# Sums of weight quarters in a Strassen-like MLP product: accumulating DMAs in place of VectorE, with the seven products in another order

## The chip, the cores and the metric

The kernel runs on one core of one Trainium2 chip. The metric is device time in microseconds of one execution. Besides the time there is a trace of one profiled execution, with every instruction of the engines: TensorE (PE; its weight loads are counted apart as PEld), VectorE (DVE), ScalarE (ACT), GpSimd (POOL), and SyncE (SP), which here only issues DMAs. POOL and ACT can issue DMAs as well.

## What is computed

One layer of a hybrid decoder: 16 meta tokens and 512 sequence positions of width 1024 pass through pooling and a state-space branch, gates and an output product; then comes a squared-ReLU MLP, and a final normalisation. The change lies in the MLP:

```python
v = rmsnorm(h, mlp_norm_w[i])
hid = jax.nn.relu(v @ w_ff1[i])          # 512 x 4096 for the positions that are kept
h = h + (hid * hid) @ w_ff2[i]           # 4096 -> 1024
```

All of it is float32. The kernel takes each float32 matrix apart into a high part that PE multiplies fast (type fp32r) and a low remainder (`hi` and `lo`), and forms a product from three matmuls: high by high, high by low, low by high.

## The kernel before

All weights come as one DRAM tensor `w` of blocks of 128 x 1024 float32 (512 KB), laid out in the order in which the kernel takes them; `nblk[0]` counts the blocks taken. SP loads a block into one of three `raw` tiles (line 68); ACT casts it to `whi` (line 69) and DVE subtracts to `wlo` (line 70); there are four `whi` and four `wlo` tiles.

The MLP stage has two kinds of work, woven into each other.

- The first product: 32 tiles `ff1_tile(c, f)`, 24 matmuls of 128 x 512 each (lines 86 to 88) into a bank `pf`, then relu and square on ACT (lines 708, 709). After the fourth tile of a group `c`, sums and differences of its quarters are formed on DVE (lines 724 to 727), and everything is taken apart into `hh` and `hl`. Six tiles run ahead; the others serve as fillers (`filler()`) between the products below.
- The second product: the depth of 4096 is taken in eight slices `c`. For the first seven, the product of the two-by-two quarters of activations and weights is formed from seven products instead of eight (Winograd's form of Strassen's method). Each product is `prod(...)`, 12 matmuls of 128 x 512 (lines 742 to 744). Four quarters of weights are loaded per slice, by `quarter` (SP, line 685), into tiles of a pool of six: `b11`, `b12`, `b22`, `b21`. The trace calls them all `b`, and the third sum tile `t`. The seven right-hand sides are b11, b22 and b21 on their own and four sums: t1 = b11 + b12, t2 = t1 + b22, b12 + b22, and t2 + b21. The four sums are formed by DVE in `sum_of` (line 764). Each right-hand side goes through `split` (ACT line 692 into `shi`, DVE line 693 into `slo`, in the same four-deep pool as `whi` and `wlo`).

The products are named after the activations' side: A11, S2, S3, A22, S4, A12 and S1. A11, S2, S3 and A22 accumulate one onto another in the PSUM tile `alpha` (two banks); S4 starts `alpha` anew. After each of these five, DVE adds or subtracts `alpha` onto the result `ht` (`onto`, line 754). The next product in `alpha` can begin only after that. A12 accumulates over all slices in `p2` (shown as `p`), S1 in two banks `q5` (shown as `q`), which in the last of the seven slices is added onto `ht` by four operations of 512 columns. The eighth slice is an ordinary product (line 849), followed by the final normalisation and the store.

The order of each engine's instructions isn't the code's order. The framework plans it once, at build time: from its own costs it follows what each engine would be doing and gives it the earliest instruction in the code whose inputs and buffers it expects to be ready. On the chip each engine then keeps to that order and waits on semaphores; it cannot pass over an instruction that waits. A tile's buffer comes free when its last reader has finished. The text speaks of a block: one of the seven slices with its seven products and the fillers among them, four in blocks 1 to 5 and three in the sixth and the seventh.

Of the kernel before, what the change touches and what calls it, by code (L numbers as in the profile page):

```python
# [9 lines left out]
F32 = mybir.dt.float32  # L10
# [4 lines left out]
P = 128  # L15
# [30 lines left out]
def kernel(ctx: ExitStack, tc, xT, x, w, vec, fnw, out):  # L46
    nc = tc.nc
    act, dve, pe, pool = nc.scalar, nc.vector, nc.tensor, nc.gpsimd
# [8 lines left out]
    nblk = [0]  # L57
# [70 lines left out]
    def psum2(name):  # L128
        return psa.tile([P, 1024], F32, tag="mm", name=name)

    def psum1(name):
        return psb.tile([P, 512], F32, tag="s", name=name)
# [71 lines left out]
    for i in range(2):  # L204
        c = slice(i * HALF, (i + 1) * HALF)
# [11 lines left out]
    def dtile(name):  # L217
        return dp.tile([P, W], F32, name=name)

    v, e, s, s2, pl, dt, acs = (dtile(n) for n in ("dv", "de", "ds", "ds2", "dpl", "ddt", "dacs"))  # L220
# [22 lines left out]
    for c in (slice(0, P), slice(P, W)):  # L243
        n = c.stop - c.start
# [342 lines left out]
    for d in range(NK):  # L587
        ps = psum2(f"pup{d}")[:, :SEQ]
        wh, wl = block()
        for n, k in enumerate(ks):  # L590
            c = slice(k * P, (k + 1) * P)
# [35 lines left out]
    for half in range(2):  # L627
# [5 lines left out]
        for kk in range(4):  # L633
            wh, wl = block()
            for k2 in range(2):
                k = 2 * kk + k2
                c = slice(k2 * 512, (k2 + 1) * 512)
# [4 lines left out]
        c = slice(half * 512, (half + 1) * 512)  # L642
# [19 lines left out]
    qp = ctx.enter_context(tc.tile_pool(name="qp", bufs=6, side="left", reuse_waits="tile"))  # L662
# [14 lines left out]
    A12, A22, A11, S1, S2, S4, S3 = range(7)  # L677
    NC = 8
    rel = {}

    def quarter(tag):
        b = nblk[0]
        nblk[0] += 1
        t = qp.tile([P, 1024], F32, tag="quarter", name=f"{tag}{b}")
        nc.sync.dma_start(t, w[b])
        return t

    def split(src):
        hi = wp.tile([P, 1024], F32R, tag="whi", name=f"shi{nsplit[0]}")
        lo = wp.tile([P, 1024], F32R, tag="wlo", name=f"slo{nsplit[0]}")  # L690
        nsplit[0] += 1
        act.copy(hi, src)  # L692
        dve.tensor_tensor(lo, src, hi.bitcast(F32), op=ALU.subtract)  # L693
        return hi, lo
# [3 lines left out]
    def ff1_tile(c, f):  # L698
        ps = psum1(f"pf{c}_{f}")
        wh, wl = block()  # L700
        for k in range(NK):
            ks = slice(k * P, (k + 1) * P)
            mm3(ps, (wh[:, ks], wl[:, ks]), (vh[k], vl[k]), k == 0, k == NK - 1)
        if f == 0:
            rel[c] = tmp.tile([P, 2, 4, 256], F32, tag="relu", name=f"r{c}")
        p, i = f // 2, f % 2
        r = rel[c][:, p, 2 * i : 2 * i + 2, :].rearrange("p s t -> p (s t)")
        act.activation(r, ps, AF.Relu)
        act.activation(r, r, AF.Square)
        if f < 3:  # L710
            return
        r = rel[c]
        hh = hid.tile([P, 2, 7, 256], F32R, tag="hh", name=f"hh{c}")
        hl = hid.tile([P, 2, 7, 256], F32R, tag="hl", name=f"hl{c}")
        if c == NC - 1:
            act.copy(hh[:, :, :4, :], r)
            dve.tensor_tensor(hl[:, :, :4, :], r, hh[:, :, :4, :].bitcast(F32), op=ALU.subtract)
            rel[c] = (hh, hl)
            return

        act.copy(hh[:, :, :3, :], r[:, :, :3, :])
        dve.tensor_tensor(hl[:, :, :3, :], r[:, :, :3, :], hh[:, :, :3, :].bitcast(F32), op=ALU.subtract)
        s = tmp.tile([P, 2, 4, 256], F32, tag="sums", name=f"s{c}")
        dve.tensor_tensor(s[:, :, 0, :], r[:, :, 3, :], r[:, :, 1, :], op=ALU.subtract)
        dve.tensor_tensor(s[:, :, 1, :], s[:, :, 0, :], r[:, :, 2, :], op=ALU.subtract)
        dve.tensor_tensor(s[:, :, 2, :], r[:, :, 0, :], s[:, :, 1, :], op=ALU.add)
        dve.tensor_tensor(s[:, :, 3, :], r[:, :, 2, :], r[:, :, 3, :], op=ALU.subtract)
        act.copy(hh[:, :, 3:, :], s)
        dve.tensor_tensor(hl[:, :, 3:, :], s, hh[:, :, 3:, :].bitcast(F32), op=ALU.subtract)
        rel[c] = (hh, hl)  # L730

    def prod(ps, c, seg, wt, first, last, ts=(0, 1)):

        hh, hl = rel[c]
        wh, wl = wt
        for t in ts:
            for p in range(2):
                st = slice(t * P, (t + 1) * P)
                a = (hh[:, p, seg, st], hl[:, p, seg, st])
                cs = slice(p * 512, (p + 1) * 512)  # L740
                f, l = first and p == 0, last and p == 1
                pe.matmul(ps[t], a[0], wh[:, cs], start=f, stop=False, skip_group_check=True)  # L742
                pe.matmul(ps[t], a[0], wl[:, cs], start=False, stop=False, skip_group_check=True)  # L743
                pe.matmul(ps[t], a[1], wh[:, cs], start=False, stop=l, skip_group_check=True)  # L744

    def onto(T, half, pst, op, t=None):

        cs = slice(half * 512, (half + 1) * 512)
        if t is None:
            o = ht[:, 2 * T : 2 * T + 2, cs]  # L750
            src = pst.rearrange("p (t d) -> p t d", t=2)
        else:
            o, src = ht[:, 2 * T + t, cs], pst
        dve.tensor_tensor(o, o, src, op=op)  # L754

    ADD, SUB = ALU.add, ALU.subtract
    alpha, p2 = psum2("alpha"), psum2("p2")
    av = [alpha[:, :512], alpha[:, 512:]]
    p2v = [p2[:, :512], p2[:, 512:]]
    q5v = [psum1(f"q5_{t}") for t in range(2)]  # L760

    def sum_of(a, b, name, out=None):
        t = out if out is not None else qp.tile([P, 1024], F32, tag="quarter", name=name)
        dve.tensor_tensor(t, a, b, op=ADD)
        return t

    def squares(t, c, n):
# [23 lines left out]
    def filler():  # L791
        if order:
            ff1_tile(*order.pop(0))

    for c in range(NC - 1):
        b11, b12, b22, b21 = (quarter(n) for n in ("b11_", "b12_", "b22_", "b21_"))
        z, e = c == 0, c == NC - 2
        prod(av, c, A11, split(b11), True, False)
        onto(0, 0, alpha, ADD)
        t1 = sum_of(b11, b12, "", b11)  # L800
        t2 = sum_of(t1, b22, f"t2_{c}")
        filler()
        prod(av, c, S2, split(t2), False, False)
        onto(0, 1, alpha, SUB)
        filler()
        prod(av, c, S3, split(sum_of(b12, b22, "", b12)), False, False)
        onto(1, 1, alpha, SUB)
        filler()
        prod(av, c, A22, split(sum_of(t2, b21, "", t2)), False, True)
        onto(1, 0, alpha, ADD)  # L810
        if e:
            prod(q5v, c, S1, split(t1), z, True)
            for t in range(2):
                onto(0, 1, q5v[t], ADD, t)
                onto(1, 1, q5v[t], ADD, t)
        elif c < NC - 3:
            filler()
        prod(av, c, S4, split(b22), True, True)
        onto(0, 1, alpha, ADD)
        prod(p2v, c, A12, split(b21), z, False)  # L820
        if not e:
            prod(q5v, c, S1, split(t1), z, False)
    assert not order


    c = NC - 1
# [5 lines left out]
    for t in range(4):  # L832
        T, st = t // 2, slice((t % 2) * P, (t % 2 + 1) * P)
        n = 0
        for half in range(2):
            parts = [(0, 512)] if half == 0 or t < 3 else [(0, 256), (256, 256)]
            for a, m in parts:
# [4 lines left out]
                for k, seg in ((1, (A11, 3)[T]), (0, (A12, A22)[T])):  # L842
                    wh, wl = wq[k, half]
                    for p in range(2):
                        x0 = p * 512 + a
                        f = i == 0 and not (T == 0 and half == 0)
# [151 lines left out]
```

## Time and profile before

| | |
|---|---|
| median of 3 runs | 1034.95 us (1034.86 to 1035.31) |
| profiled execution | 1035.26 us |
| its span, first to last instruction | 1033.5 us |
| mean granted PE clock | 0.998 |
| busy: PE, PEld | 1019.6 us, 880.2 us |
| busy: DVE, ACT, POOL | 714.2 us, 542.3 us, 9.9 us |
| read from HBM | 102.95 MB |
| MLP stage, first filler to last matmul | 697.8 to 1028 us |

A line of the timeline gives an instruction's start and duration, the engine, the line of the code, the operation, the tiles written and read, and in brackets the idle time of the engine before it and what released it. Matmuls overlap in the pipeline: each shows 0.39 us but the next one starts 0.23 us later. A line of groups gives the same for all instructions of one kind, with their count and duration (least, median, most). A DMA's landing time counts from its issue to the moment that its data is there.

### The profile page before, as it was taken

The page shows a single profiled execution, that of the slowest core. Times are in us where ns is not written, and L with a number is a line of the kernel's source. Part 1 is how long each engine was busy: PE and PEld are TensorE (multiplying, and loading weights), DVE is VectorE, ACT ScalarE, POOL GpSimd, SP SyncE. Part 2 cuts the span into 40 slices and gives each one's busy share as a digit, 9 for nine tenths or more (in the row PEclk, how much of TensorE's full clock was granted, in tenths as well). Part 3 has the DMA queues.
Part 4 walks back from the last instruction along what each step waited for, and adds up shares of the span by engine and source line. Part 5 has one row for each costly group of instructions (what it writes and reads, how often), then busy time and mean ns, then how long its engine had stood idle before and what let it go on. Part 6 is the DMA issues. An engine that isn't in the chain of part 4 may idle for free.

```text
span 1033.5 us, 13995 instructions
## 1 busy us (share of the span) xinstructions
PE 1019.6 (99%) x5700; PEld 880.2 (85%) x5700; DVE 714.2 (69%) x932; ACT 542.3 (52%) x706; POOL 9.9 (1%) x24
## 2 busy tenths in 40 slices
PE   7999999999999999999999999999999999999997
PEld 7889988898879898988998888878888888888886
DVE  7978787687636586878664345645686676776866
ACT  7675968586627349573443123344555354454444
POOL 0100000000000000000000000000000000000000
PEclk9999999999999999999999999999999999999999
DMA  6343041414332321413232323533324323334112
GB/s 229 110 140 103 21 164 37 148 47 137 102 112 73 103 101 41 146 59 111 77 107 95 102 81 102 204 126 122 99 82 123 103 81 122 102 102 123 42 41 82
DMA packets 29424, 106.01 MB, mean 103 GB/s; under 512 B 3312, under 2 KB 4272, under 8 KB 28336
## 3 DMA queue, kind: packets, MB, share of 16 engines
q1 hardware_dynamic: 26640, 93.14, 28.8%
q0 software_dynamic: 2000, 11.08, 2.9%
q8 instruction: 45, 0.74, 0.3%
q10 hardware_dynamic: 720, 0.91, 0.3%
q14 instruction: 19, 0.16, 0.0%
HBM read 102.95 MB, written 2.16 MB: 102 GB/s over the span
## 4 chain that ended last, share of the span: by engine, by line
PE 97%; DVE 1%; DMA 1%; ACT 0%; issue 0%; SPq 0%; ACTq 0%
PE px L138 6%; PE px L141 6%; PE px L139 6%; PE pf L86 6%; PE pf L87 6%; PE pf L88 6%; PE alpha L742 3%; PE alpha L743 3%; PE alpha L744 3%; PE pz L139 3%; PE pz L141 3%; PE pz L138 3%; PE py L416 2%; PE pso L86 2%; PE pp L141 2%; PE pp L139 2%
## 5 line engine op out<-in xcount | busy, mean ns | idle before, releaser
L69 ACT CAST whi<-raw 128x1024 fp32r<-128x1024 f32 (+2 forms) x141 | 145.4, 1037 | 274.3 <-PE pf L87 61.3
L70 DVE TENSOR_TENSOR wlo<-raw,whi 128x1024 fp32r<-128x1024 f32 (+2 forms) x141 | 169.8, 1206 | 151.5 <-ACT whi L69 151.5
L138 PE MATMUL px<-uh,whi 128*128 128x264 f32 (+1 forms) x448 | 121.0, 291 | 0.7 <-DVE ct L280 0.7
L139 PE MATMUL px<-ul,whi 128*128 128x264 f32 (+1 forms) x448 | 118.2, 284 | 0.0
L86 PE MATMUL pf<-vh,whi 128*128 128x512 f32 x256 | 99.7, 389 | 1.2 <-DVE vl L651 1.2
L87 PE MATMUL pf<-vl,whi 128*128 128x512 f32 x256 | 99.6, 389 | 0.0
L88 PE MATMUL pf<-vh,wlo 128*128 128x512 f32 x256 | 99.6, 389 | 0.0
L141 PE MATMUL px<-uh,wlo 128*128 128x264 f32 (+1 forms) x448 | 91.5, 285 | 0.0
L138 PEld LDWEIGHTS px<-uh,whi 128*128 128x128 f32 x448 | 84.6, 189 | 2.8 <-issue 2.6
L139 PEld LDWEIGHTS px<-ul,whi 128*128 128x128 f32 x448 | 84.4, 188 | 0.3
L141 PEld LDWEIGHTS px<-uh,wlo 128*128 128x128 f32 x448 | 69.4, 188 | 0.3 <-issue 0.3
L693 DVE TENSOR_TENSOR slo<-b,shi 128x1024 fp32r<-128x1024 f32 x35 | 42.7, 1220 | 31.6 <-ACT shi L692 31.6
L692 ACT CAST shi<-b 128x1024 fp32r<-128x1024 f32 x35 | 36.7, 1050 | 51.9 <-PE pf L87 36.5
L86 PEld LDWEIGHTS pf<-vh,whi 128*128 128x128 f32 x256 | 48.1, 188 | 11.5 <-DVE vl L651 1.5
L88 PEld LDWEIGHTS pf<-vh,wlo 128*128 128x128 f32 x256 | 48.0, 188 | 10.0
L87 PEld LDWEIGHTS pf<-vl,whi 128*128 128x128 f32 x256 | 48.1, 188 | 9.8
L742 PE MATMUL alpha<-shi,hh 128*128 128x512 f32 x140 | 54.6, 390 | 0.0
L743 PE MATMUL alpha<-slo,hh 128*128 128x512 f32 x140 | 54.5, 389 | 0.0
L744 PE MATMUL alpha<-shi,hl 128*128 128x512 f32 x140 | 54.5, 389 | 0.0
L754 DVE TENSOR_TENSOR ht<-ht,alpha 128x1024 f32<-128x1024 f32 x35 | 42.6, 1216 | 6.1 <-PE alpha L744 6.1
L139 PE MATMUL pz<-ul,whi 128*128 128x512 f32 x112 | 44.3, 395 | 0.0
L141 PE MATMUL pz<-uh,wlo 128*128 128x512 f32 x112 | 44.1, 394 | 0.0
(330 smaller groups left out, 2395.8 us busy)
## 6 DMA issues: line engine op xcount, KB each, us to landing
raw<-in_w SPq DMA_DIRECT2D x137, 512.0 KB, 3.6
b<-in_w SPq DMA_DIRECT2D x28, 512.0 KB, 3.5
abc<-acs_d POOLq DMA_DIRECT2D x8, 1024.0 KB, 7.2
xt<-in_xT SPq DMA_DIRECT2D x8, 264.0 KB, 6.2
ht<-in_x POOLq DMA_DIRECT2D x4, 512.0 KB, 5.0
w<-in_w SPq DMA_DIRECT2D x4, 512.0 KB, 3.5
out_dram<-out SPq DMA_DIRECT2D x4, 320.0 KB, 2.4
raw<-in_w SPq DMA_DIRECT2D x2, 384.0 KB, 5.5
```

What stands on the lines that cost most here:

```text
L69: act.copy(hi[:, c], raw[:, c])
L70: dve.tensor_tensor(lo[:, c], raw[:, c], hi[:, c].bitcast(F32), op=ALU.subtract)
L86: pe.matmul(ps, ah, bh, start=first, stop=False)
L87: pe.matmul(ps, ah, bl, start=False, stop=False)
L88: pe.matmul(ps, al, bh, start=False, stop=last)
L138: pe.matmul(o, wh, rhs[0][k][:, c], start=k == 0, stop=False)
L139: pe.matmul(o, wh, rhs[1][k][:, c], start=False, stop=False)
L141: pe.matmul(o, wl, rhs[0][k][:, c], start=False, stop=k == NK - 1)
L693: dve.tensor_tensor(lo, src, hi.bitcast(F32), op=ALU.subtract)
L742: pe.matmul(ps[t], a[0], wh[:, cs], start=f, stop=False, skip_group_check=True)
L743: pe.matmul(ps[t], a[0], wl[:, cs], start=False, stop=False, skip_group_check=True)
L744: pe.matmul(ps[t], a[1], wh[:, cs], start=False, stop=l, skip_group_check=True)
```

## The change

Per block of the loop over the first seven slices:

- Two of the four loaded tiles get new names, `run` (b11) and `t3` (b12); `b22` and `b21` stay. SP's loads are the same.
- `sum_of` is gone, with the 28 DVE additions. In its place `plus` issues from POOL a DMA that reads a block of `w` from DRAM again and adds it onto a tile in SBUF (`accum_op=ADD`). There are four per block: b22 onto `t3`; and b12, b22, b21 onto `run`, one after the other, so that `run` is in turn b11, t1, t2 and t2 + b21. Each step on `run` comes after the `split` of the value before it.
- The tile for t2 of its own is gone: four tiles of the pool of six per block instead of five.
- The order of the products in the code: A11, S1, filler, S2, filler, S3, filler, A22, (filler), A12, S4. Before: A11, filler, S2, filler, S3, filler, A22, (filler), S4, A12, S1.
- In the last of the seven blocks the additions of `q5` onto `ht` come right after S1, now the second product.

```diff
-    def sum_of(a, b, name, out=None):
-        t = out if out is not None else qp.tile([P, 1024], F32, tag="quarter", name=name)
-        dve.tensor_tensor(t, a, b, op=ADD)
+    def plus(t, b):
+
+        nc.gpsimd.dma_start(t, w[b], accum_op=ADD)
         return t
...
     for c in range(NC - 1):
-        b11, b12, b22, b21 = (quarter(n) for n in ("b11_", "b12_", "b22_", "b21_"))
+        n0 = nblk[0]
+        run, t3, b22, b21 = (quarter(n) for n in ("run_", "t3_", "b22_", "b21_"))
         z, e = c == 0, c == NC - 2
-        prod(av, c, A11, split(b11), True, False)
+        plus(t3, n0 + 2)
+        prod(av, c, A11, split(run), True, False)
         onto(0, 0, alpha, ADD)
-        t1 = sum_of(b11, b12, "", b11)
-        t2 = sum_of(t1, b22, f"t2_{c}")
-        filler()
-        prod(av, c, S2, split(t2), False, False)
-        onto(0, 1, alpha, SUB)
-        filler()
-        prod(av, c, S3, split(sum_of(b12, b22, "", b12)), False, False)
-        onto(1, 1, alpha, SUB)
-        filler()
-        prod(av, c, A22, split(sum_of(t2, b21, "", t2)), False, True)
-        onto(1, 0, alpha, ADD)
+        w1 = split(plus(run, n0 + 1))
+        prod(q5v, c, S1, w1, z, e)
         if e:
-            prod(q5v, c, S1, split(t1), z, True)
             for t in range(2):
                 onto(0, 1, q5v[t], ADD, t)
                 onto(1, 1, q5v[t], ADD, t)
-        elif c < NC - 3:
+        w2 = split(plus(run, n0 + 2))
+        plus(run, n0 + 3)
+        filler()
+        prod(av, c, S2, w2, False, False)
+        onto(0, 1, alpha, SUB)
+        filler()
+        prod(av, c, S3, split(t3), False, False)
+        onto(1, 1, alpha, SUB)
+        filler()
+        prod(av, c, A22, split(run), False, True)
+        onto(1, 0, alpha, ADD)
+        if c < NC - 3:
             filler()
+        prod(p2v, c, A12, split(b21), z, False)
         prod(av, c, S4, split(b22), True, True)
         onto(0, 1, alpha, ADD)
-        prod(p2v, c, A12, split(b21), z, False)
-        if not e:
-            prod(q5v, c, S1, split(t1), z, False)
     assert not order
```

## The prediction

> **What bounds the kernel now.** I read the page's head first, then the busy time of the engines block by block in the stage that the change touches, then the order of the matmuls there, and last how early each weight tile is ready.
>
> ```profile
> span 1033.5 us, 13995 instructions
> ...
> PE 1019.6 (99%) x5700; PEld 880.2 (85%) x5700; DVE 714.2 (69%) x932; ACT 542.3 (52%) x706; POOL 9.9 (1%) x24
> ```
>
> TensorE (PE) is busy 99% of the span. The stage of the change runs in blocks of 40.8 us; here are two of them, with the busy microseconds of PE, PEld, DVE, ACT and POOL, the granted clock and the DMA share:
>
> ```profile
> 771.30:812.10 40.80, 40.80 (x181) 33.78 (x180) 29.52 (x27) 19.29 (x21) 0.00 (x0) 1.00 0.34 103
> 812.10:852.90 40.80, 40.80 (x181) 33.78 (x180) 29.53 (x27) 19.28 (x21) 0.00 (x0) 1.00 0.34 104
> ```
>
> PE has no idle time at all there, at a granted clock of 1.00. The matmuls stay the same in number and shape, so there is nothing to gain on PE: VectorE (DVE), which the change relieves, is busy 29.5 us of 40.8 and nobody on PE waits for it. The question is only whether the new order opens holes in PE. For that I need the tempo. The first matmul of each product, from A22 of one block to the first filler of the next (`alpha`, `p`, `q` are the product banks, `pf` is a filler):
>
> ```profile
> 755.01 0.39 PE L742 MATMUL alpha<-shi,hh 128*128 128x512 f32 x1
> ...
> 757.74 0.39 PE L86 MATMUL pf<-vh,whi 128*128 128x512 f32 x1
> ...
> 763.17 0.39 PE L742 MATMUL alpha<-shi,hh 128*128 128x512 f32 x1
> ...
> 765.89 0.39 PE L742 MATMUL p<-shi,hh 128*128 128x512 f32 x1
> ...
> 768.62 0.39 PE L742 MATMUL q<-shi,hh 128*128 128x512 f32 x1
> ...
> 771.34 0.39 PE L742 MATMUL alpha<-shi,hh 128*128 128x512 f32 x1
> ...
> 774.05 0.39 PE L86 MATMUL pf<-vh,whi 128*128 128x512 f32 x1
> ```
>
> A product takes 2.72 us (763.17 to 765.89), a filler 5.43 us (757.74 to 763.17). Seven products and four fillers make 7 x 2.72 + 4 x 5.43 = 40.8 us.
>
> How far ahead are the weights? There are four `whi`/`wlo` buffers, so a split can start when the product four places earlier ends. The split that waits for A22 (ACT's cast, then DVE's subtraction, in time order on each engine):
>
> ```profile
> 757.93 1.05 ACT L692 CAST shi<-b 128x1024 fp32r<-128x1024 f32 x1 [0.64 <-PE alpha L744]
> ```
> ```profile
> 757.62 1.22 DVE L693 TENSOR_TENSOR slo<-b,shi 128x1024 fp32r<-128x1024 f32 x1
> 758.76 1.22 DVE L754 TENSOR_TENSOR ht<-ht,alpha 128x1024 f32<-128x1024 f32 x1
> 759.89 1.22 DVE L693 TENSOR_TENSOR slo<-b,shi 128x1024 fp32r<-128x1024 f32 x1
> ```
>
> A22's matmuls end at 757.74; the cast starts at 757.93, and its subtraction, behind two other operations of DVE, ends at 759.89 + 1.22 = 761.11. So a split is done 3.4 us after the end of the product four places before it.
>
> Engines run in an order planned ahead, not in code order. Two sums of the first block run long before the addition onto `ht` that stands above them in the code:
>
> ```profile
> 716.53 1.23 DVE L764 TENSOR_TENSOR b<-b,b 128x1024 f32<-128x1024 f32 x1
> ...
> 733.46 1.22 DVE L754 TENSOR_TENSOR ht<-ht,alpha 128x1024 f32<-128x1024 f32 x1 [0.64 <-PE alpha L744]
> ```
>
> PE too is filled this way. In the sixth block no filler stands between A22 and S4, and S4 must wait until `alpha` has been added onto `ht`:
>
> ```profile
> 961.51 0.39 PE L744 MATMUL alpha<-shi,hl 128*128 128x512 f32 x1
> 961.74 0.39 PE L742 MATMUL p<-shi,hh 128*128 128x512 f32 x1
> ...
> 963.77 0.39 PE L742 MATMUL p<-shi,hh 128*128 128x512 f32 x1
> 964.02 0.50 PE L742 MATMUL alpha<-shi,hh 128*128 128x512 f32 x1
> ```
> ```profile
> 959.08 1.05 ACT L692 CAST shi<-b 128x1024 fp32r<-128x1024 f32 x1
> ```
> ```profile
> 961.62 1.22 DVE L693 TENSOR_TENSOR slo<-b,shi 128x1024 fp32r<-128x1024 f32 x1
> 962.76 1.21 DVE L754 TENSOR_TENSOR ht<-ht,alpha 128x1024 f32<-128x1024 f32 x1
> ```
>
> Ten matmuls of the following product were put into the hole (961.74 to 964.0), and all but about 0.1 us of it vanished.
>
> **The change, part by part.**
>
> *Sums removed.* 28 operations on line 764 go:
>
> ```profile
> L692 ACT CAST shi<-b x35: 1042/1049/1055, 714.2 to 994.5; 128x1024 fp32r<-128x1024 f32 x35
> L693 DVE TENSOR_TENSOR slo<-b,shi x35: 1215/1220/1227, 715.3 to 995.6; 128x1024 fp32r<-128x1024 f32 x35
> ...
> L764 DVE TENSOR_TENSOR b<-b,b x14: 1214/1222/1226, 716.5 to 970.9; 128x1024 f32<-128x1024 f32 x14
> L764 DVE TENSOR_TENSOR t<-b,b x7: 1217/1219/1226, 717.8 to 966.4; 128x1024 f32<-128x1024 f32 x7
> L764 DVE TENSOR_TENSOR t<-t,b x7: 1217/1224/1226, 727.4 to 975.5; 128x1024 f32<-128x1024 f32 x7
> ```
>
> 28 x 1.22 = 34 us leave DVE, 4.9 of its 29.5 us per block. All of it lay beside a PE without idle time: worth 0.
>
> *28 accumulating DMAs added*, 512 KB each, on POOL, which does nothing in this stage. Issuing costs POOL 0.53 us each, 2.1 us per block: 0. What counts is D, the time from issue to landing, for which the trace has only plain transfers:
>
> ```profile
> q1 hardware_dynamic: 26640, 93.14, 28.8%
> q0 software_dynamic: 2000, 11.08, 2.9%
> ...
> b<-in_w SPq DMA_DIRECT2D x28, 512.0 KB, 3.5
> abc<-acs_d POOLq DMA_DIRECT2D x8, 1024.0 KB, 7.2
> ...
> ht<-in_x POOLq DMA_DIRECT2D x4, 512.0 KB, 5.0
> ```
> ```profile
> L625 POOL DMA_DIRECT2D ht<-in_x x4: 527/528/530, 645.1 to 646.7; - x4
> ...
> DMA to landing us min/median/max: 3.9/5.0/8.7
> ```
> ```profile
> fw<-in_fnw POOLq DMA_DIRECT2D x1, 512.0 KB, 9.4
> ```
>
> The lowest end is 3.5 us (SP's plain load), the highest 9.4 us (the last of five POOL transfers in a crowd). A POOL transfer of this size takes 3.9 us at best, 5.0 in the median. An addition must also fetch what stands in the destination, so I charge a second pass over the bytes: q0 moved 11.08 MB in 2.9% of 16 engines' span, 0.029 x 1033.5 / 11.08 = 2.7 us per MB, or 1.4 us for 0.524 MB; by q1's rates 1.7 us. That makes 3.9 + 1.4 = 5.3 to 5.0 + 1.7 = 6.7. I take D = 6.0, halfway, between the rows of one and of two passes (5.0 for 512 KB, 7.2 for 1,024 KB).
>
> The same choice weighed against a rule: by the plain row alone (5.0 us) the sum below would come to nothing. The Trainium skill, "Collectives: The Full Stack", section "The bandwidth ceiling: the fold count and why AG ≠ RS ≠ AR", says that an add in the DMA engines is slowed not by the arithmetic but by needing two source reads, which halves the rate. By that rule D would be 5.0 plus one pass, about 6.5, and the sum about 9 us; no run here shows it yet.
>
> *The chain run, run+b12, run+b12+b22, run+b12+b22+b21.* Each sum overwrites `run`, so each DMA waits until both halves of the split before it have read it, and the next split waits for its landing. Count from the end of A22. The next block's A11 is now the product four places on (F4, A12, S4, A11), so its split is done at 3.4. The first DMA lands at 3.4 + D, and cast and subtraction (1.05 + 1.22) make S1's weights ready at 5.7 + D. S4 ends at 5.43 + 2 x 2.72 = 10.9.
>
> *S4 last, A11 next, both in `alpha`.* Before, A12 and S1 (5.4 us) covered the addition of `alpha` onto `ht`; now nothing in the code stands between. As in the sixth block, I expect PE's order to be filled with what is next: S1's matmuls, which use other banks. Then S1 is due at 10.9, not after A11, and D may be 5.2. With D = 6.0 PE waits 6.0 - 5.2 = 0.8 us at each boundary. S2's weights are ready at 5.7 + 2D + 2.3 = 20.0, due at 10.9 + 2 x 2.72 + 5.43 = 21.7: no wait. The third sum has S2, two fillers and S3 in front of it: no wait. t3's sum waits for nothing but its own load, and is used only after A11, S1, S2 and two fillers: no wait. On ACT and DVE, behind a late S1 split, stand the filler's cast and the next `onto`, which then move with PE.
>
> Boundaries: blocks 1 to 5 into the next, five of this form, 5 x 0.8 = 4.0 us. The sixth into the seventh has no filler F4: its split starts with the end of the third filler (959.01; cast 959.08) and ends at 961.62 + 1.22 = 962.84, 3.8 us later. S1 is ready at 3.8 + 6.0 + 2.3 = 12.1, S4 ends at 8.2; S1 cannot fill, the filler and A11 do (until 16.3). S2 is ready at 12.1 + 8.3 = 20.4 and due at 8.2 + 2 x 2.72 + 5.43 = 19.0: 1.4 us. The first block has six fillers of lead: 0.
>
> *Smaller edits.* A12 before S4 takes away the 0.1 us of the sixth block. q5's additions in the last block come earlier, beside fillers: 0. Four `quarter` tiles per block instead of five in six buffers: SP's loads start earlier, never later; SP's queue gets no new wait but the readers of `run`. The added traffic, 14.7 MB and as much read again, takes some 4 x 2.8 = 11 us more per block of DMA time, 0.34 to about 0.6: collisions stretch D by up to a load's pass of 1.7 us, inside the range of D.
>
> Sum: 4.0 + 1.4 - 0.1 = +5.3 us. The profiled execution took 1035.26 us, span 1033.5 and 1.8 around it; the median of the runs is 1034.95, 0.3 lower. 1035.26 + 5.3 = 1040.6, on the median 1040.3; I say **1040.5**. Each us of D above 5.2 costs 5 + 2 = 7 us, so D from 5.3 to 6.7 gives 1035.5 to 1046.
>
> **The rivals.**
> 1. *Hidden.* The DMA lands within 5.2 us of issue (for it: 3.9 and 5.0 on plain rows; against: the destination must be read), or the filler's matmuls rather than S1's are planned into the hole behind S4, and S1 follows A11, due 4 us later; then S2 decides, at 8.0 + 2D = 21.7, D = 6.9. Time 1035.0. It is the case on the other side: not slower.
> 2. *Slow accumulation*, D of 8 to 9.4 (for it: 8.7 and 9.4 in the rows; against: those were in a crowd). 5 x 2.8 + 2 x 2.7 = 19 us gives 1054; at 9.4, 5 x 4.2 + 2 x 4.1 = 29, 1064 at least, since then S2 is late everywhere as well.
> 3. *Nothing fills the hole behind S4.* PE waits for one addition of `alpha`, 1.2 us or, behind a subtraction, 2.3 us as from 961.74 to 964.02, six times: 7 to 14 us, 1042 to 1049, whatever D is up to 9. Against it: the sixth block was filled.
> 4. *Faster.* There are 0.1 us of PE idle time to take in the blocks; 2 us would have to come from the tail.
>
> **How the numbers follow.** No change can be told from one within 0.2% (2 us). Chances: the sum with D of 5.3 to 6.7: 0.38 (of it 0.03 below +2 us); hidden 0.26; slow accumulation 0.23, a third of it above 1065; not filled 0.10; faster 0.03. Slower 0.35 + 0.23 + 0.10 = 0.68, same 0.29, faster 0.03. The range 1034.5 to 1064 leaves out about 0.1 above and little below; the likeliest case alone has 1035.5 to 1046.
>
> **What would show it.** In the profile after: DMA issues of `run` and `t3` on POOL with D about 6 us; line 764 gone from DVE and about 25 us busy per block; PE waits of 0.5 to 1.5 us at S1's first matmuls (bank `q`) behind each S4, released by the subtraction of S1's split; blocks of about 41.6 us. PE waits at `alpha` released by the addition onto `ht` would mean rival 3; blocks of 40.8 rival 1; waits at S2 as well rival 2. The prediction is wrong if D is under 5.2 or over 6.7, or if the hole is filled otherwise.

## The result, and the profile after

The changed kernel takes 1077.9 us (median of 4 runs, 1076.7 to 1081.8). Against the kernel before, run beside it, the ratio is 1.042 (95% interval 1.041 to 1.043). That is 43 us slower. The prediction was 1040.5 us with a range of 1034.5 to 1064: the sign was right, the time lies outside the range.

The head of the page of the changed kernel, with one of its DMA queues and the two groups of accumulating DMAs (the last column is the median time from issue to landing):

```profile
span 1075.0 us, 14022 instructions
...
PE 1035.0 (96%) x5700; PEld 885.6 (82%) x5700; DVE 681.8 (63%) x904; ACT 540.3 (50%) x706; POOL 34.1 (3%) x52
...
q0 software_dynamic: 6032, 25.76, 11.0%
...
run<-in_w POOLq DMA_DIRECT2D x21, 512.0 KB, 5.7
...
t<-in_w POOLq DMA_DIRECT2D x7, 512.0 KB, 6.9
```

The edits are all there: DVE has 28 operations and 32 us less, POOL 28 instructions and 24 us more, and the DMAs land in the time that was forecast for them, or 0.2 us above it. But TensorE (PE), with the same 5700 matmuls, is busy 96% instead of 99%. Two of the blocks, by the busy time of the engines (columns as in the prediction):

```profile
821.21:867.95 46.74, 43.30 (x181) 34.72 (x180) 24.98 (x23) 19.05 (x21) 3.45 (x4) 0.96 0.54 135
867.95:915.95 48.00, 43.96 (x181) 35.09 (x180) 24.62 (x23) 19.05 (x21) 3.44 (x4) 0.93 0.50 132
```

The same 181 matmuls that took 40.8 us take 46.7 and 48.0 us. PE has idle time now (3.4 and 4.0 us), and even its busy time has grown, by 2.5 to 3.2 us at a granted clock of 0.96 and 0.93. The waits of PE, longest in total first (us in total, times, longest):

```profile
PE pf L86 <- ACT whi L69: 14.7, 7, 3.6
...
PE q L742 <- ACT shi L692: 4.1, 2, 3.8
PE pf L88 <- DVE wlo L70: 3.1, 5, 0.7
PE q L743 <- DVE slo L693: 1.9, 5, 0.8
PE q L744 <- DVE hl L729: 1.6, 1, 1.6
```

The largest is not at any product of the changed chain but at `pf`: the **fillers** wait for their own cast `whi`, whose input was loaded long before. Why, the timelines of ACT, DVE and POOL at the first boundary show (start, duration, instruction, and in brackets the idle time before it and what ended it):

```profile
774.48 1.05 ACT L692 CAST shi<-run 128x1024 fp32r<-128x1024 f32 x1 [3.28 <-DMA run<-in_w]
782.66 1.04 ACT L692 CAST shi<-run 128x1024 fp32r<-128x1024 f32 x1 [7.13 <-DMA run<-in_w]
783.61 1.99 ACT L69 CAST whi<-raw 128x1024 fp32r<-128x1024 f32 x2
```
```profile
783.74 1.22 DVE L693 TENSOR_TENSOR slo<-run,shi 128x1024 fp32r<-128x1024 f32 x1 [5.82 <-ACT shi L692]
784.88 1.22 DVE L70 TENSOR_TENSOR wlo<-raw,whi 128x1024 fp32r<-128x1024 f32 x1
```
```profile
767.96 0.86 POOL L764 DMA_DIRECT2D run<-in_w  x1 [33.93 <-DVE slo L693]
...
777.08 0.87 POOL L764 DMA_DIRECT2D run<-in_w  x1 [6.76 <-DVE slo L693]
```

The first DMA is issued at 767.96 and S1's cast starts at 774.48; the second is issued when S1's split has read `run`, at 777.08, and S2's cast starts at 782.66. ACT stood still for 7.13 us before it, with the filler's cast next in its order, and that one runs at 783.61, right behind. PE at the next boundary shows what this costs:

```profile
826.99 0.39 PE L744 MATMUL q<-shi,hl 128*128 128x512 f32 x1
829.84 0.50 PE L86 MATMUL pf<-vh,whi 128*128 128x512 f32 x1 [2.46 <-ACT whi L69]
...
831.28 0.51 PE L88 MATMUL pf<-vh,wlo 128*128 128x512 f32 x1 [0.71 <-DVE wlo L70]
831.63 0.50 PE L86 MATMUL pf<-vh,whi 128*128 128x512 f32 x1
831.93 0.63 PE L87 MATMUL pf<-vl,whi 128*128 128x512 f32 x1
832.35 0.63 PE L88 MATMUL pf<-vh,wlo 128*128 128x512 f32 x1
...
835.27 0.39 PE L86 MATMUL pf<-vh,whi 128*128 128x512 f32 x1
```

S1 and A11 are over at 826.99; the filler's first matmul waits until 829.84, its third, which needs `wlo`, until 831.28. After that the matmuls start 0.42 us apart instead of 0.23, up to 835.27: PE runs at about half pace for 3.6 us.

Where the 41.5 us of span went, from the starts of all matmuls of this stage (what a start is late beyond 0.23 us after the one before; more than 0.26 us of lateness is counted as a hole): 21.2 us in holes ahead of fillers, 9.8 us in holes ahead of S1's matmuls, 10.1 us in 61 matmuls that are late by less (41 of them, 7.9 us, start 0.38 to 0.43 us apart as above; the other 20 are about 0.1 us late, most of them right behind a hole). Together 41.1 us. Before, the same count gives 0.2 us.

### The profile page after: what moved, and what is told of

The parts are those of the page before. It is cut to its first block, busy times and chain, and to the rows that moved or that the text cites. A ratio compares the mean times of both kernels' runs of the same rounds, so it can differ in the third digit from the quotient of the medians.

```text
span 1075.0 us, 14022 instructions
## 1 busy us (share of the span) xinstructions
PE 1035.0 (96%) x5700; PEld 885.6 (82%) x5700; DVE 681.8 (63%) x904; ACT 540.3 (50%) x706; POOL 34.1 (3%) x52
## 3 DMA queue, kind: packets, MB, share of 16 engines
q0 software_dynamic: 6032, 25.76, 11.0%
## 5 line engine op out<-in xcount | busy, mean ns | idle before, releaser
L86 PE MATMUL pf<-vh,whi 128*128 128x512 f32 x256 | 102.7, 401 | 16.0 <-ACT whi L69 14.7
L88 PE MATMUL pf<-vh,wlo 128*128 128x512 f32 x256 | 102.4, 400 | 3.1 <-DVE wlo L70 3.1
L87 PE MATMUL pf<-vl,whi 128*128 128x512 f32 x256 | 101.8, 398 | 0.0
L693 DVE TENSOR_TENSOR slo<-run,shi 128x1024 fp32r<-128x1024 f32 x28 | 34.2, 1222 | 83.7 <-ACT shi L692 83.7
L692 ACT CAST shi<-run 128x1024 fp32r<-128x1024 f32 x28 | 29.4, 1049 | 84.7 <-DMA run<-in_w 66.5
```

The costliest lines, as they stand in the source:

```text
L86: pe.matmul(ps, ah, bh, start=first, stop=False)
L87: pe.matmul(ps, ah, bl, start=False, stop=False)
L88: pe.matmul(ps, al, bh, start=False, stop=last)
```

## The experiments

Three theories were tested. **A**: two landings in series stand in ACT's and DVE's fixed order, and what costs is the work queued behind the instruction that waits for them. **B**: it is the new order of the products, above all S4 directly ahead of A11 in the bank `alpha`, whoever forms the sums. **C**: it is the DMAs' own work, 14.7 MB more of it beside SP's loads. The edits are shown against the changed kernel, where nothing else is said. Times are medians, ratios are to the kernel before run beside them, with their 95% interval.

| kernel | us | ratio |
|---|---|---|
| changed kernel | 1077.9 | 1.042 (1.041 to 1.043) |
| order_dve: new order, sums by DVE | 1036.0 | 1.001 (1.000 to 1.002) |
| plain_dma: DMAs that don't add | 1045.1 | 1.010 (1.008 to 1.011) |
| filler_cast_first | 1048.2 | 1.013 (1.011 to 1.014) |
| s4_then_a12 | 1075.8 | 1.039 (1.038 to 1.041) |
| t3_dve | 1078.7 | 1.041 (1.039 to 1.043) |
| before_plus_dmas: order and sums of before | 1035.4 | 1.000 (0.999 to 1.001) |
| spread | 1082.0 | 1.043 (1.042 to 1.045) |
| spread_double | 1154.9 | 1.115 (1.114 to 1.117) |
| spread_pin | 1047.4 | 1.012 (1.010 to 1.014) |
| spread_pin_t3 | 1045.8 | 1.010 (1.009 to 1.012) |
| spread_pin2 | 1043.3 | 1.009 (1.007 to 1.011) |

**The order alone.** The new order of products, with the four sums formed by DVE in `sum_of`, as in the kernel before:

```diff
-        plus(t3, n0 + 2)
...
-        w1 = split(plus(run, n0 + 1))
+        w1 = split(sum_of(run, t3, "", run))
...
-        w2 = split(plus(run, n0 + 2))
-        plus(run, n0 + 3)
+        t2 = sum_of(run, b22, f"t2_{c}")
+        sum_of(t3, b22, "", t3)
+        w2 = split(t2)
+        sum_of(t2, b21, "", t2)
...
-        prod(av, c, A22, split(run), False, True)
+        prod(av, c, A22, split(t2), False, True)
```

> The new order of the products, with the four sums of a block formed by VectorE as before. Theory A (the two DMA round trips in series between A11's split and S2's split, with the filler's cast behind S2's split on ACT, make the holes): no split waits for a DMA any more, S1's weights are ready long before A11 ends and fill the hole behind S4; 1035 us, within 3. Theory B (the order itself: S4 next to A11 in alpha, S1 so early in the block): 1050 to 1078 us, PE waits at q or alpha behind S4 as in the changed kernel.

Measured: 1036.0 us, within 0.2% of before. S4 ahead of A11 in one bank costs nothing as long as the weights come in time, and theory B falls: the order matters only together with the late sums. Since this kernel and the changed one differ in who forms the sums, 42 of the 43 us belong to that.

**The DMAs without the addition.** The transfers stay where they are and only overwrite, so the sums are left out and the output is not the reference's:

```diff
-        nc.gpsimd.dma_start(t, w[b], accum_op=ADD)
+        nc.gpsimd.dma_start(t, w[b])
```

> The changed kernel with plain DMAs from POOL into the same tiles at the same places: they overwrite instead of adding, so the sums are left out. Theory A: with D near 4.5 us instead of about 6.2, the filler's cast, which comes two DMAs after A22's end, is early by 2 x 1.7 = 3.4 us per block; PE waits of 43 us fall to 5 to 18, time 1040 to 1053 us. Theory C (the added traffic and its collisions with SP's loads, not the addition, sets D): D stays above 5.5 us and the time above 1065 us.

The DMA group of `run` on that kernel's page, and the largest waits of its PE at the products and fillers:

```profile
run<-in_w POOLq DMA_DIRECT2D x21, 512.0 KB, 3.8
```
```profile
PE pf L88 <- DVE wlo L70: 2.6, 5, 0.7
PE pf L86 <- ACT whi L69: 1.4, 3, 0.8
```

Landing in 3.8 instead of 5.7 us takes 33 of the 43 us away; what is left is again waits of the fillers. Two landings stand in the path of each filler, so 1.9 us less per landing is 3.8 us per boundary, which is about what the hole at `pf` was (2.5 + 0.9). The excess isn't proportional to the landing time: two thirds of the landing leave less than a quarter of the excess. That it begins at a certain landing time is the reading that fits; only these two were run.

**The filler's cast ahead of S2's.** Nothing is changed but the place of one filler in the code, ahead of the second DMA and S2's split:

```diff
+        filler()
         w2 = split(plus(run, n0 + 2))
         plus(run, n0 + 3)
-        filler()
```

> The changed kernel with the first filler of a block written ahead of S2's accumulating DMA and split, so that its tiles and its cast come before S2's on ACT. Order of the matmuls on PE nearly unchanged. Theory A: the waits at pf (21.7 us and most of the half-rate matmuls behind them) go, the waits at q behind S4 stay: 1045 to 1056 us. Theory B (order of the products): no change, 1070 to 1080 us.

1048.2 us: 30 us come back, although all 28 DMAs are there and the landings are as long. ACT's timeline at the first boundary, and the waits of PE:

```profile
769.71 1.05 ACT L692 CAST shi<-run 128x1024 fp32r<-128x1024 f32 x1 [2.95 <-DMA run<-in_w]
770.66 1.04 ACT L69 CAST whi<-raw 128x1024 fp32r<-128x1024 f32 x1
778.31 1.05 ACT L692 CAST shi<-run 128x1024 fp32r<-128x1024 f32 x1 [6.61 <-DMA run<-in_w]
779.26 1.05 ACT L69 CAST whi<-raw 128x1024 fp32r<-128x1024 f32 x1
```
```profile
PE alpha L742 <- DVE ht L754: 3.0, 5, 0.6
...
PE pf L86 <- ACT whi L69: 0.2, 1, 0.2
```

The first filler's cast now runs at 770.66, ahead of S2's wait of 6.61 us and not behind it, and PE begins that filler at 778.32 with no wait. The cast behind S2's, at 779.26, is the second filler's, which PE begins only at 786.48. The wait of `pf` for `whi` fell from 14.7 to 0.2 us. PE's order at this boundary is the same as in the changed kernel. What remains are holes ahead of S1's matmuls (6.0 us by the starts of the matmuls), at `alpha` (3.9) and 2.8 us of smaller lateness: the landing on the path to S1, as in the prediction's sum, and on DVE S4's addition onto `ht`, which now stands behind S1's subtraction and the filler's `wlo`.

**A12 behind S4 again.** The last part of the new order undone:

```diff
-        prod(p2v, c, A12, split(b21), z, False)
         prod(av, c, S4, split(b22), True, True)
         onto(0, 1, alpha, ADD)
+        prod(p2v, c, A12, split(b21), z, False)
```

> The changed kernel with S4 ahead of A12 again, so that A12 covers the addition of alpha onto ht and S1 isn't needed to fill a hole. Theory A: the filler still waits for two DMAs after A22's end, so what is saved at q is lost again at pf: 1070 to 1085 us. Theory B: 7 to 14 us less than the changed kernel, 1062 to 1071 us, and no PE waits at pf.

1075.8 us, 2 us less than the changed kernel, the intervals of the ratios overlapping. The waits of PE move from one place to another: 12.3 us, ten times, at `alpha` for additions onto `ht`, and 5.2 us at `pf`. A second product behind S4 does not bring the weights sooner; it is not the place of S4 that costs.

**The third sum by DVE again.** b22 is added onto `t3` by DVE, so the first DMA on `run` does not share its time with another one:

```diff
-        plus(t3, n0 + 2)
+        dve.tensor_tensor(t3, t3, b22, op=ADD)
```

> The changed kernel with t3's sum formed by VectorE, so that no other accumulating DMA is issued right behind the first one on run. If the collision with t3's DMA stretches the first landing (6.4 us against 5.6): 0.8 us per block less, 1070 to 1074 us. If not: 1075 to 1079 us.

1078.7 us: no gain. The collision of the two DMAs at the boundary isn't what makes the kernel slow.

**The DMAs alone.** The kernel before, its order and DVE's sums untouched, with the 28 accumulating DMAs added onto a tile that nobody reads (against the kernel before):

```diff
+    scratch = qp.tile([P, 1024], F32, tag="scratch", name="scratch", bufs=1)
+    dve.memset(scratch, 0.0)
     for c in range(NC - 1):
+        n0 = nblk[0]
+        for b in (2, 1, 2, 3):
+            nc.gpsimd.dma_start(scratch, w[n0 + b], accum_op=ADD)
```

> The kernel before, with the 28 accumulating DMAs added onto a tile that nobody reads; its own sums stay on VectorE. Theory A2: nothing waits for them, 1034 to 1037 us. Theory C (their traffic delays SP's loads, or their issue disturbs the engines): above 1040 us.

The group on its page:

```profile
scratch<-in_w POOLq DMA_DIRECT2D x28, 512.0 KB, 5.7
```

28 DMAs with the same landing time of 5.7 us, and 1035.4 us, against 1035.4 without them. They run one behind another from 701 to 886 us, closer together than in the changed kernel. SP's loads of the quarters now take 4.4 us to land instead of 3.5, but PE waits for none of them. Theory C falls: neither the traffic nor POOL's issuing costs any time that can be measured. Only the wait for the landing is left.

**The fillers spread out.** If the two landings must have more work in front of them, a filler between A11 and S1 and one between S1 and S2 should hide both:

```diff
         onto(0, 0, alpha, ADD)
+        filler()
         w1 = split(plus(run, n0 + 1))
         prod(q5v, c, S1, w1, z, e)
...
+        filler()
         w2 = split(plus(run, n0 + 2))
         plus(run, n0 + 3)
-        filler()
         prod(av, c, S2, w2, False, False)
...
-        filler()
+        if c < NC - 3:
+            filler()
         prod(av, c, A22, split(run), False, True)
         onto(1, 0, alpha, ADD)
-        if c < NC - 3:
-            filler()
```

> All accumulating DMAs of the changed kernel, with the fillers spread along the chain: A11, filler, S1, filler, S2, filler, S3, (filler), A22, A12, S4. Theory A: counted from the end of the fourth filler, S1's weights are ready at 5.7 + D = 12 us and due at 16.3, S2's at 8.1 + 2D = 20.5 and due at 24.5, so no hole in PE: 1034 to 1037 us, same as before within 0.2%. Theory C (the accumulating DMAs cost something of their own, by traffic or collisions): above 1040 us.

1082.0 us: the forecast of theory A missed by some 45 us. The waits at `pf` were all but gone, and a new one had come. The largest wait of this kernel's PE, and then the timelines of PE, DVE and POOL at the first boundary:

```profile
PE alpha L742 <- DVE ht L754: 34.5, 6, 7.1
```
```profile
771.39 0.39 PE L744 MATMUL alpha<-shi,hl 128*128 128x512 f32 x1
...
773.20 0.39 PE L87 MATMUL pf<-vl,whi 128*128 128x512 f32 x1
779.60 0.80 PE L742 MATMUL alpha<-shi,hh 128*128 128x512 f32 x1 [6.01 <-DVE ht L754]
```
```profile
777.19 1.23 DVE L693 TENSOR_TENSOR slo<-run,shi 128x1024 fp32r<-128x1024 f32 x1 [8.46 <-ACT shi L692]
778.33 1.21 DVE L754 TENSOR_TENSOR ht<-ht,alpha 128x1024 f32<-128x1024 f32 x1
```
```profile
765.75 0.86 POOL L764 DMA_DIRECT2D t<-in_w  x1 [28.52 <-DVE slo L693]
766.28 1.20 POOL L764 DMA_DIRECT2D run<-in_w  x1
```

S4's last matmul starts at 771.39. DVE is idle at that time, but the addition of `alpha` onto `ht` runs only at 778.33, since S1's subtraction stands ahead of it in DVE's order and waits for the landing (issued at 766.28, 9.8 us before S1's cast at 776.11, the two DMAs in flight together). A11 can't start before that addition. So the theory was right on what waits, and I had looked at one queue only: a waiting split holds up what is behind it on ACT **and** on DVE. Amended to A2: any order is good in which nothing that PE needs soon stands behind a split that waits for a DMA.

**The landings doubled.** As spread, with each accumulating DMA issued twice (the quarter is added twice, so the output is not the reference's):

```diff
         nc.gpsimd.dma_start(t, w[b], accum_op=ADD)
+        nc.gpsimd.dma_start(t, w[b], accum_op=ADD)
```

> The kernel of label spread with each accumulating DMA issued twice, one after the other (the result is wrong by the second addition), so that D is about 12 us. Theory A: S1 ready at 17.7 us, due at 16.3; S2 ready at 8.1 + 2 x 12 = 32, due at 25.9: some 7 us of waits per block and a stretch of half-rate matmuls behind each, 1070 to 1100 us. Rival (the slack in spread is larger than counted, since PE's order adapts): below 1050 us.

1154.9 us, 73 us above spread, more than expected. A second landing in each step is added to a path that is already the longest, with 37 us of holes ahead of S1 (spread has none there), 44 at `alpha` (spread: 37) and 9 at `p`. Together with before_plus_dmas this says: the price is set by how late the landing is on the path, and is zero off it.

**A2 tested: only DVE's order.** As spread, and S1's subtraction is held behind S4's addition onto `ht` and behind A11's by an order constraint (`onto` now returns its instruction). No operation is added or removed:

```diff
-        onto(0, 0, alpha, ADD)
+        added = onto(0, 0, alpha, ADD)
         filler()
-        w1 = split(plus(run, n0 + 1))
+        plus(run, n0 + 1)
+        with tc.issue_after(added.ins):
+            w1 = split(run)
```

> The kernel of label spread, with S1's subtraction held, in the planned order of VectorE, behind the addition of A11's alpha onto ht (an order only, no wait), so that no addition of alpha stands behind a subtraction that waits for a DMA. Theory A2 (the plan counts on a shorter landing than the chip gives, and what it queued behind the waiting cast or subtraction makes the holes): the waits of A11 for alpha (34.5 us in spread) go, and with D of 6 to 10 S1 is ready at 12 to 16 us and due at 16.3; 1034 to 1040 us. Theory C (cost of the accumulating DMAs themselves): above 1060 us.

DVE of this kernel at the same boundary, then in the sixth block:

```profile
771.82 1.22 DVE L754 TENSOR_TENSOR ht<-ht,alpha 128x1024 f32<-128x1024 f32 x1 [3.08 <-PE alpha L744]
776.15 1.22 DVE L754 TENSOR_TENSOR ht<-ht,alpha 128x1024 f32<-128x1024 f32 x1 [3.11 <-PE alpha L744]
778.19 1.23 DVE L693 TENSOR_TENSOR slo<-run,shi 128x1024 fp32r<-128x1024 f32 x1 [0.82 <-ACT shi L692]
...
959.51 1.22 DVE L693 TENSOR_TENSOR slo<-run,shi 128x1024 fp32r<-128x1024 f32 x1 [5.16 <-ACT shi L692]
...
964.76 1.21 DVE L754 TENSOR_TENSOR ht<-ht,alpha 128x1024 f32<-128x1024 f32 x1
```

Both additions now precede the subtraction, and the time falls from 1082.0 to 1047.4 us: 35 of 47 us come back by an order held on one engine. The plan of the others moves a little with it (ACT takes a filler's relu ahead of S2's cast, at 780.00 and not at 789.39), but the wait that is gone is the one at `alpha` that A2 named. That carries A2. It still misses the forecast by 7 us. The rest has the same form: in the sixth block, the subtraction of `run` for A22 (959.51) comes after 5.16 us of waiting for its cast; behind it stand the sums of a relu group and then S2's addition (964.76), and S3 waits 5.1 us for that on PE.

**The same, with t3 by DVE.** spread_pin, and:

```diff
-        plus(t3, n0 + 2)
+        dve.tensor_tensor(t3, t3, b22, op=ADD)
```

> As spread_pin, with t3's sum by VectorE, so that the first DMA on run isn't issued beside t3's. Theory A2: D near 5.6 instead of up to 10 us, S1 ready at 11.3 of 16.3 us; same time as spread_pin within 2 us if that has no waits at q, else 1034 to 1036 us.

1045.8 us, 1.6 us less than without, the intervals of the ratios overlapping. Having the first DMA alone is worth little here too.

**A22's split held back too.** spread_pin, and A22's split is held behind S2's addition (`added`) and behind the square of the filler ahead of S2 (`second`):

```diff
+        with tc.issue_after(added.ins), tc.issue_after(second.ins):
+            w3 = split(run)
-        prod(av, c, A22, split(run), False, True)
+        prod(av, c, A22, w3, False, True)
```

> As spread_pin, with the split before A22 held as well: its cast behind the square of the filler before S2, its subtraction behind the addition of S2's alpha onto ht (orders only). In spread_pin the one large hole left (5.2 us in the sixth block, A11's bank alpha waiting for an addition queued behind that subtraction) goes by theory A2, with its half-rate matmuls: 1036 to 1041 us. If the rest of spread_pin's 10 to 12 us is a cost of the DMAs themselves: 1045 us or more.

The waits of PE in the stage:

```profile
PE alpha L743 <- DVE ht L755: 2.1, 2, 1.7
PE p L744 <- DVE slo L693: 1.7, 1, 1.7
```

1043.3 us (six runs, 1041.0 to 1048.3, which overlap with those of spread_pin), a little above what was expected. The trace shows that the 5.1 us hole is gone; waits of 2 us each are left in the sixth block, which has no fourth filler to cover anything. No version came below the kernel before, which has only 0.2 us of lateness among its matmuls in this stage: with all holes gone, what is left is the same 5700 matmuls.

## Why the prediction was wrong, and where it was right

**Right.** Nothing is gained by relieving DVE: order_dve has 715.1 us of DVE work, the changed kernel 681.8, and the one with more is as fast as before. POOL's issuing is free (before_plus_dmas), though it takes 0.87 us each and not 0.53. D was 5.7 us in the median for `run` and 6.9 for `t3`, where 6.0 with 5.3 to 6.7 was taken. At the boundary PE's order behind S4 was indeed filled with S1's matmuls, seven of them at 821.21 to 823.13 ahead of A11, so rival 3 (not filled) fell, and S1 waited 0.3 to 1.4 us at the first five boundaries, where 0.8 was predicted. Rival 1 (hidden) fell with that. Rival 2 (1054 to above 1064) comes closest by its time, but by the number alone: its condition, D of 8 to 9.4, did not occur (the 21 landings on `run` took 5.4 to 6.9 us).

The rule that was weighed can now be set against a run. In plain_dma, q0 moves the same 25.76 MB in 7.3% of the DMA engines' time (of a span of 1043.9 us), where the changed kernel has 11.0% of 1075.0. Less the 30.0 us of the kernel before, the added 14.68 MB took 3.1 us per MB plain and 6.0 adding: 1.9 times as much. The Trainium skill, "Collectives: The Full Stack", section "The bandwidth ceiling: the fold count and why AG ≠ RS ≠ AR", with its two source reads at half the rate, agrees with that; the page says it of a collective's ReduceScatter, and this is a local DMA. The landing grew less, by 1.5 times.

**Wrong: the step "S2's weights are ready at 5.7 + 2D + 2.3 = 20.0, due at 10.9 + 2 x 2.72 + 5.43 = 21.7: no wait".** The arithmetic on S2 itself holds, and PE never waited for S2. But ahead of S2 on PE comes a filler, due at 10.9 + 2 x 2.72 = 16.3, and its cast stands behind S2's in ACT's order. S2's cast ends at 5.7 + 2D + 1.05, the filler's at 7.8 + 2D, which is 19.8 with D = 6.0: 3.5 us after PE wants it, or 2.7 once the 0.8 at S1 has moved PE, and its subtraction on DVE comes later still. Measured were 2.5 to 3.8 us ahead of the filler and 0.6 to 0.9 ahead of its third matmul at those boundaries. The text had seen the filler's cast, in the sentence "On ACT and DVE, behind a late S1 split, stand the filler's cast and the next `onto`, which then move with PE", but put it behind S1's split and priced it at nothing. It stood behind S2's, and what stands behind a wait doesn't move with PE; PE moves with it. filler_cast_first is the test of this step: 30 us from one moved filler. The prediction's list of rivals lacked this case: rival 2 has "S2 late everywhere as well" at D above 9, while the late filler needs a D above 4.3 only (7.8 + 2D = 16.3). plain_dma, at 3.8 us, lies below that, and its waits for `whi` are 1.4 us instead of 14.7.

**Wrong: "The first block has six fillers of lead: 0".** The lead does not help against the order of DVE and ACT. S1's third matmul needs the second part of `hl` (line 729), which is queued behind S2's subtraction, and for it the second part of `hh`, whose cast (line 728, at 731.54) is queued on ACT behind S2's cast:

```profile
731.67 1.23 DVE L693 TENSOR_TENSOR slo<-run,shi 128x1024 fp32r<-128x1024 f32 x1 [2.79 <-ACT shi L692]
733.47 2.29 DVE L729 TENSOR_TENSOR hl<-s,hh 128x2048 fp32r<-128x2048 f32 x1 [0.58 <-ACT hh L728]
```

It cost two holes (0.5 and 1.8 us) and seven matmuls at half pace (1.4 us).

**Wrong in size: the boundary of the sixth block, 1.4 us.** "S1 cannot fill, the filler and A11 do" did not happen: two of S1's matmuls stand ahead of A11 in PE's order, and PE stands still from 1002.86 to 1007.07 until their cast is done. With the filler's hole of this block (966.89 to 970.59) and the half pace after each, the sixth block took 46.0 us where 35.4 were due.

**Not priced at all: the clock.** Some 8 of the 41.1 us are matmuls at half pace, after the holes. Eleven matmuls in a row at half pace, as after the hole at 1002.86, cost 2 us beside the hole itself.

The sum in terms: predicted 4.0 (S1 at five boundaries) + 1.4 (sixth) = 5.4 us; measured 9.8 us in holes ahead of S1 (4.3 of them at the sixth boundary, 1.8 and 0.5 in the first block, 3.2 at the five), 21.2 ahead of fillers, 10.1 of smaller lateness, most of it at half pace.

What stays open: that the framework plans its order with a shorter landing than the chip's is inferred from the order (it puts S2's cast ahead of the filler's, which would be right if both were ready early); its costs were not read. Of spread_pin2's remaining 8 us over before, 5 are holes by the starts and 1 smaller lateness, at a granted clock of 1.00; no further order was tried.

## What to carry to other kernels

Taking work off an engine that nobody waits for is worth nothing, and the DMA that replaces it has a latency: 5.7 us here against 1.2 us for the sum on DVE, twice in series. For each wait that a change adds, list what is queued behind the waiting instruction on **its own** engine, on every engine that the result passes through, and ask when PE needs each of these; the late product itself may never show. When a chain of waits gives a wait at a place whose input has long been there, look at the line above it in that engine's timeline, and try the order first: moving one filler, or holding one subtraction back, was worth 30 to 35 us here.

## What the runs showed of the hardware

- An accumulating DMA of 512 KB from DRAM onto SBUF lands after 5.7 us in the median, a plain one from POOL in the same place after 3.8. Issuing it takes POOL 0.87 instead of 0.53 us. Of two issued within 0.6 us of each other the later one (766.28 above) let its cast start only 9.8 us on, at 776.11. The groups of the tile `run`, with least, median and most nanoseconds of an issue, in the changed kernel and then in plain_dma:

```profile
L764 POOL DMA_DIRECT2D run<-in_w x21: 845/867/870, 716.6 to 1018.2; - x21
```
```profile
L764 POOL DMA_DIRECT2D run<-in_w x21: 527/527/530, 716.6 to 984.9; - x21
```

- Spells of half clock begin after holes of 1.8 to 4.0 us, and not after each of them. The granted clock changes on a fixed grid: the five spells of the changed kernel's MLP stage begin at 736.19, 831.77, 876.14, 971.71 and 1005.85, 28, 13, 28 and 10 times 3.41 us apart, and last 3.41 us or twice that. Two holes of nearly one length, in stretches cut along this grid (columns as above):

```profile
780.57:783.98 3.41, 1.78 (x8) 1.13 (x6) 0.24 (x1) 1.32 (x2) 0.00 (x0) 1.00 0.39 76
783.98:787.39 3.41, 1.97 (x7) 1.35 (x8) 3.41 (x4) 2.57 (x3) 0.85 (x1) 1.00 0.12 14
...
828.36:831.77 3.41, 1.22 (x4) 0.74 (x5) 2.90 (x3) 3.32 (x4) 0.86 (x1) 1.00 0.00 0
831.77:835.18 3.41, 3.41 (x10) 2.63 (x9) 2.86 (x3) 0.00 (x0) 0.00 (x0) 0.50 0.99 154
```

The hole before 784.70 (2.5 us) is divided between two stretches, PE is busy for 1.78 and 1.97 us in them, and the clock stays at 1.00. Of that before 829.84 (2.6 us), 1.5 us and a hole of 0.9 us behind it fall into one stretch, which has PE busy for 1.22 us, and the next 3.41 us run at half the clock. In this kernel's stage, PE was busy for 0.7 to 1.5 us in the stretch ahead of each spell, and for 1.8 us or more in the stretches at full clock that no spell followed. The Trainium skill, "TensorE: Matmul & The Clock Gate", section "Part 1: The HAM clock gate (the "warmup" mystery)", says that PE's activity is judged in a free-running window of about 3.4 us, with half the clock after an idle one. The grid agrees; that a whole idle window is needed is not borne out here, since windows in which PE was busy for up to 1.5 us were enough.
